# Moving weight preparation out of a state-space stage: where side work stands in the engines' queues

## The chip, the cores and the metric

The kernel runs on one core of a Trainium2 chip. The core has a matrix engine (PE, whose weight loads are listed apart as PEld), a vector engine (DVE), a scalar engine (ACT), a general engine (POOL) and an engine that here only issues transfers (SP). Each engine works through its own instructions in a fixed order and waits on semaphores for the others; transfers run on DMA engines and are issued from the queue of an engine, here SP or ACT. The metric is the device time of one execution in microseconds. A comparison of two kernels uses the median of several executions on the same chip.

## The reference: what is computed

One decoder block over 1024 positions of width 1024, in fp32. Two branches read one normalised input; they are merged by gates and projected. Then come a cross-attention into 256 memory tokens and a gated feed-forward.

```python
u = rms_norm(h, norm_mix[l])
proj = u @ w_in[l]                       # u_ssm, q, k, v, f_logit, gate_logits
y_ssm = gelu(s5_ssm(u_ssm, ...))         # state space
glu_a, glu_b = split(y_ssm @ w_glu[l], 2)
out_a = glu_a * sigmoid(glu_b)
out_b = forgetting_attention(q, k, v, f_logit + b_forget[l]) @ w_fox_o[l]
gate_a, gate_b = split(sigmoid(gate_logits), 2)
h = h + (gate_a * out_a + gate_b * out_b) @ w_mix_out[l]
h = h + memory_cross_attention(...)
f_a, f_b = split(rms_norm(h, norm_ffn[l]) @ w_ffn_in[l], 2)
h = h + (silu(f_a) * f_b) @ w_ffn_out[l]
return rms_norm(h, norm_final)
```

## The kernel before, in words

Each fp32 operand of a product is held as two parts: a high part (an ACT copy in a narrower type, L177) and a low part (the rest, a subtraction on DVE, L178); `split` makes both. Each product is three matmuls (`mm3`, L167 to L169) of 128 by 128 weights by 512 columns. Weights come through `wblock`: a load by SP into `raw`, then a split into `whi` and `wlo`.

The stages, by the time at which they stand in the profile: the normalised input and first products (0 to about 100 us); the state-space stage `stage_ssm` (about 100 to 357); the forgetting attention (to about 645); the head of `stage_tail`, in which eight blocks of the gated unit (GLU), of the attention's output product and of the merge are computed in one loop over j (about 645 to 800); the memory attention; and the feed-forward, which multiplies 2 by 2 blocks with seven products of sums of blocks instead of eight products. Those sums are taken of the weights too, so each block j of the feed-forward needs its weights in seven prepared pieces, each in a high and a low part.

**The state-space stage.** 32 gate products (16 blocks by two halves, 24 matmuls each) run one behind the other on PE. Their sigmoids run on ACT (L479) and are stored to `gate_d` by a DMA from ACT's queue (L480). Between them stands the state-space work of four groups q, set by the dictionary `todo`: before gate product 4+7q `turn_weights(q)` (transposes L1405, products L1411, and three dependent transfers `Ts<-Ts` on SP, L1418), before 5+7q `states` (the load `xg<-u_d` on SP, L1429, and its products L1436), before 8+7q the ACT copy `Tt<-Ts` (L1423), before 9+7q `out` (products `pv<-xg,Tt` L1479 and L1480, and the activation `m<-pv` L1483) and `store` (`y_d<-yh`, `y_d<-yl` on SP). A second dictionary, `jobs`, hangs side work on the gate products. One kind is for the mixer, four times over: fetch two rows of blocks of `w_mix_out` into `wk` (two buffers), add and subtract them on DVE (L507), store to `sums_d` (L511). The other is for the first two blocks of the feed-forward (`AHEAD_IN = 2`): fetch two pieces of `w_ffn_in` into the same `wk` buffers (L516), add on DVE (L525), split into `wh` (three buffers), and store to `w_d` (L533). The feed-forward reads `w_d` at about 947 to 999 us (L890).

**The tail's loop.** For each j: a load of the GLU's weights, the value products and their copies on DVE (`sg<-mm`, L1162), the gate products with a sigmoid on ACT (`sb`, L1167) and a multiply on DVE (L1168), the state-space gate on POOL (L1175), then `fox_part(j)`: the product of the attention's output (PSUM bank `pv`), a gate and an add on DVE (`gb`, L612, and `sg<-sg,gb`, L613), splits into `A11`, and for j below 4 a subtraction, a split into `S3` and a store `am_d<-sg`.

**What sets the order.** A scheduler puts each engine's instructions into a fixed order before the launch. `tc.issue_after(ins)` holds what is written inside it behind `ins`, but only those instructions that are on the same engine as `ins`: with a mark on ACT, the DVE and SP instructions inside it are not held. In `stage_ssm` the mark is the gate's sigmoid, an ACT instruction:

```python
            with B.tc.issue_after(mark[-1].ins):   # L560
                for g in jobs.pop(i):
                    g()
```

Of the kernel before, what the change touches and what calls it, by code (L numbers as in the profile page):

```python
# [19 lines left out]
P = 128  # L20
# [270 lines left out]
AHEAD_IN = 2  # L291


@with_exitstack
def hybrid_block_kernel(ctx: ExitStack, tc: tile.TileContext, x, mem, norm_mix, w_in, b_forget,
# [19 lines left out]
    w_d = B.dram.tile([AHEAD_IN, 7, P, D], F32, name="w_d")  # L315
# [3 lines left out]
    with tc.tile_pool(name="ssm", bufs=1) as sp:  # L319
        s5 = S5(B, sp, lam_re[0], lam_im[0], log_dt[0], b_re[0], b_im[0], c_re[0], c_im[0], d_skip[0])  # L320
        with tc.tile_pool(name="xin", bufs=1) as xp:
            stage_in(B, xp, s5, x, mem, norm_mix[0], norm_mem_kv[0], w_in, w_mem_kv, uT, u_d, kv_d)
        with tc.tile_pool(name="qp", bufs=1, reuse_waits="tile") as qp:
            stage_ssm(B, s5, qp, uT, w_in, gate_d, u_d, y_d, w_mix_out, sums_d, w_ffn_in, w_d)
# [8 lines left out]
    with tc.tile_pool(name="st2", bufs=1, reuse_waits="tile") as s2:  # L333
        stage_tail(B, big, s2, sh, x, glu, aT, gate_d, kv_d, sums_d, w_d, w_fox_o, w_mix_out, norm_mem_q[0], w_mem_q,
# [125 lines left out]
def stage_ssm(B, s5, qp, uT, w_in, gate_d, u_d, y_d, w_mix_out, sums_d, w_ffn_in, w_d):  # L460
# [29 lines left out]
    V, mw, kept = B.V, {}, {}  # L490

    def wide():
        return [qp.tile([P, D], F32, tag="wk", bufs=2, name="wk") for _ in range(2)]

    def mix_fetch(k):
        mw[k] = wide()
# [16 lines left out]
    def ffn_fetch(j):  # L513
        mw["f", j] = wide()
        for w_, c in zip(mw["f", j], (0, FH)):
            S.dma_start(w_.rearrange("p (k c) -> p k c", k=8),  # L516
                        w_ffn_in[:, c + j * P:c + (j + 1) * P].rearrange("(k p) c -> p k c", p=P))

    def ffn_part(j, n):

        (a1, a2), (b1, b2) = [(w_[:, :512], w_[:, 512:]) for w_ in mw["f", j]]
        src, adds = {1: (a1, ()), 2: (a2, ()), 5: (a1, ((a2, b2), (a1, b1), (b1, b2))), 6: (a1, ((a2, a1), (a1, b2))),
                     7: (b1, ()), 3: (b2, ()), 4: (a2, ())}[n]
        for o, i in adds:
            V.tensor_add(o, o, i)  # L525
        kept[j, n] = [qp.tile([P, 512], F32R, tag="wh", bufs=3, name="wh") for _ in range(2)]
        B.split(*kept[j, n], src)

    def ffn_keep(j, n):
        i, h = {1: (0, 0), 2: (0, 1), 5: (2, 0), 6: (2, 1), 7: (4, 0), 3: (5, 0), 4: (5, 1)}[n]  # L530
        for m, t_ in enumerate(kept.pop((j, n))):
            o = 512 * (m if n == 7 else h)
# [22 lines left out]
    for i, f in enumerate(gates):  # L555
# [3 lines left out]
        if i in jobs:  # L559
            with B.tc.issue_after(mark[-1].ins):  # L560
                for g in jobs.pop(i):
                    g()


def stage_tail(B, big, s2, sh, x, glu, aT, gate_d, kv_d, sums_d, w_d, w_fox_o, w_mix_out, g_mq, w_mem_q, w_mem_o, g_ffn,
# [94 lines left out]

    for j in range(8):
# [3 lines left out]
        glu.rest(j)  # L665
        if j == 6:
# [472 lines left out]
class Glu:  # L1139
# [24 lines left out]
    def sigmoid(self, j, h):  # L1164
# [3 lines left out]
        self.B.V.tensor_mul(dst, dst, sb)  # L1168
# [717 lines left out]
```

## Time and profile before

| | us |
|---|---|
| median of 3 runs | 1619.14 (1617.86 to 1624.33) |
| the profiled execution | 1617.85 |
| its span, from the first to the last instruction | 1616.1 |
| PE busy in it | 1538.5 |
| DVE busy | 1071.5 |
| ACT busy | 670.2 |
| mean clock granted to PE | 0.975 |

The profiled execution took 1.75 us beside its span. A row of a timeline reads: start, length, engine, line, operation and tiles (out<-in), shape, count, and in brackets how long the engine had been idle before it and what it waited for. A row with "w_d<-wh" as releaser means that the landing of that store set it free. A row of the windows reads: stretch, length, then for PE, PEld, DVE, ACT and POOL the busy time with the count of instructions, then the clock granted to PE, the busy share of the DMA engines and GB/s.

### The profile page before, as it was taken

To read this page: it belongs to the slowest core of one execution; us is meant where nothing else is said; L and a number is where in the kernel's file an instruction comes from. 1 tells how busy PE (TensorE), PEld (TensorE's weight loads), DVE (VectorE), ACT (ScalarE), POOL (GpSimd) and SP (SyncE) were. 2 spreads that over 40 slices of the span, in tenths; PEclk is the share of its full clock that TensorE was granted. 3 is DMA by queue.
4 is the path that set the end of the run, shared out by engine and by line. 5 is a ranking of instruction groups with operands and counts; after the bars stand their busy time and mean duration, and the time that the engine had idled before them with its cause. 6 is when DMAs were issued, how large, how long until landed. Compare 5 with 4: busy or idle time off the path is not lost.

```text
span 1616.1 us, 20580 instructions
## 1 busy us (share of the span) xinstructions
PE 1538.5 (95%) x7301; PEld 1267.2 (78%) x7301; DVE 1071.5 (66%) x1902; ACT 670.2 (41%) x1193; POOL 237.7 (15%) x323
## 2 busy tenths in 40 slices
PE   6899799889999999999999998999999999999997
PEld 5688688779877667888878887888888888788886
DVE  5757666254477777878685687776776676466555
ACT  5522333332366664323355565333333333244342
POOL 3024434020011111410011210100010000000001
PEclk8999999899999989999999999999999999999999
DMA  8747654964113364556532168444445444796642
GB/s 261 150 99 180 198 139 146 190 193 125 14 35 56 61 167 138 180 178 218 186 92 79 66 208 316 152 151 150 156 157 168 158 150 145 263 391 230 196 157 104
DMA packets 204886, 258.70 MB, mean 160 GB/s; under 512 B 36248, under 2 KB 127288, under 8 KB 204272
## 3 DMA queue, kind: packets, MB, share of 16 engines
q1 hardware_dynamic: 200176, 249.01, 51.2%
q10 hardware_dynamic: 4608, 8.39, 1.4%
q8 instruction: 57, 0.93, 0.2%
q14 instruction: 45, 0.37, 0.1%
HBM read 176.08 MB, written 83.20 MB: 160 GB/s over the span
## 4 chain that ended last, share of the span: by engine, by line
PE 73%; DVE 9%; DMA 8%; POOL 3%; ACT 3%; issue 3%; SPq 1%; DVEq 0%; POOLq 0%; ACTq 0%
PE mm L943 15%; PE pv L943 7%; PE mm L167 6%; PE mm L169 6%; PE mm L168 6%; PE mm L1080 4%; PE sc L943 4%; PE sc L1080 3%; PE pv L1080 3%; DMA w_d<-wh 2%; PE mm L652 2%; PE sc L167 2%; PE sc L169 2%; PE sc L168 2%; PE misc L1080 1%
## 5 line engine op out<-in xcount | busy, mean ns | idle before, releaser
L178 DVE TENSOR_TENSOR wlo<-raw,whi 128x1024 fp32r<-128x1024 f32 (+2 forms) x126 | 134.1, 1067 | 109.4 <-ACT whi L177 108.9
L177 ACT CAST whi<-raw 128x1024 fp32r<-128x1024 f32 (+2 forms) x127 | 115.6, 914 | 143.8 <-PE mm L168 42.2
L167 PE MATMUL mm<-uh,whi 128*128 128x512 f32 x344 | 138.5, 403 | 3.0 <-ACT whi L177 3.0
L169 PE MATMUL mm<-uh,wlo 128*128 128x512 f32 x344 | 136.0, 396 | 0.4 <-DVE wlo L178 0.4
L168 PE MATMUL mm<-ul,whi 128*128 128x512 f32 x344 | 136.2, 396 | 0.0
L178 DVE TENSOR_TENSOR ol<-or,oh 128x1024 fp32r<-128x1024 f32 x73 | 89.3, 1223 | 70.7 <-ACT oh L177 69.6
L177 ACT CAST oh<-or 128x1024 fp32r<-128x1024 f32 x73 | 76.8, 1052 | 103.7 <-PE mm L1080 35.2
L975 POOL TENSOR_TENSOR g<-a,c 128x512 f32<-128x512 f32 x22 | 35.6, 1619 | 393.6 <-ACT a L974 374.1
L167 PEld LDWEIGHTS mm<-uh,whi 128*128 128x128 f32 x344 | 65.7, 191 | 15.5 <-ACT whi L177 3.5
L169 PEld LDWEIGHTS mm<-uh,wlo 128*128 128x128 f32 x344 | 65.5, 190 | 14.9 <-DVE wlo L178 1.5
L168 PEld LDWEIGHTS mm<-ul,whi 128*128 128x128 f32 x344 | 65.8, 191 | 11.0
L196 POOL TENSOR_TENSOR r<-ms,mhalf 128x1 f32<-128x1 f32 (+1 forms) x30 | 18.8, 629 | 374.8 <-DVE ms L192 345.8
L1705 POOL TENSOR_TENSOR pl<-pf,ph 128x512 fp32r<-128x512 f32 (+1 forms) x32 | 36.8, 1151 | 249.8 <-DVE ph L1704 204.7
L1702 ACT ACTIVATE pf<-sc 128x512 f32<-128x512 f32 (+1 forms) x96 | 46.4, 490 | 53.1 <-DVE sc L1698 31.1
L943 PE MATMUL pv<-S3h,we 128*128 128x512 f32 x176 | 58.1, 389 | 0.0
L167 PE MATMUL sc<-uh,whi 128*128 128x512 f32 x104 | 41.5, 399 | 0.0
L1080 PE MATMUL mm<-oh 128*128 128x512 f32 x106 | 41.2, 389 | 0.0
L1080 PE MATMUL mm<-ol,oh 128*128 128x512 f32 x106 | 41.2, 389 | 0.0
L1080 PE MATMUL mm<-oh,ol 128*128 128x512 f32 x106 | 41.2, 389 | 0.0
L1708 DVE TENSOR_TENSOR pl<-pf,ph 128x512 fp32r<-128x512 f32 (+2 forms) x64 | 35.5, 557 | 8.6 <-ACT ph L1707 7.8
L169 PE MATMUL sc<-uh,wlo 128*128 128x512 f32 x104 | 41.0, 394 | 0.0
L168 PE MATMUL sc<-ul,whi 128*128 128x512 f32 x104 | 41.0, 394 | 0.0
(675 smaller groups left out, 4594.6 us busy)
## 6 DMA issues: line engine op xcount, KB each, us to landing
or<-c_d SPq DMA_DIRECT2D x77, 256.0 KB
wo<-in_w_ffn_out_dram SPq DMA_DIRECT2D x22, 512.0 KB
c_d<-g SPq DMA_DIRECT2D x44, 256.0 KB
t_d<-wo SPq DMA_DIRECT2D x44, 256.0 KB
or<-t_d SPq DMA_DIRECT2D x44, 256.0 KB
raw<-in_w_ffn_in_dram SPq DMA_DIRECT2D x20, 512.0 KB
rawb<-in_w_ffn_in_dram SPq DMA_DIRECT2D x20, 512.0 KB
raw<-in_w_in_dram SPq DMA_DIRECT2D x18, 512.0 KB
```

What stands on the lines that cost most here:

```text
L167: T.matmul(ps, lh, rh, start=first, stop=False)
L168: T.matmul(ps, lh, rl, start=False, stop=False)
L169: T.matmul(ps, ll, rh, start=False, stop=last)
L177: self.A.copy(hi, src)
L178: (self.G if pool_lo else self.V).tensor_sub(lo, src, f32(hi))
L652: T.matmul(ps, l_[:, k, :], r_[:, k, :], start=n in (1, 2, 7) and kk == k == m == 0, stop=kk == k == 1 and m == 2, skip_group_check=True)
L943: T.matmul(ps, l_[:, k, :], r_, start=first and k == 0 and i == 0, stop=k == 3 and i == 2, skip_group_check=True)
L975: G.tensor_mul(g[:, 512:], a1, c1)
L1080: T.matmul(ps, l_[:, gi], r_[:, 512:], start=n < 3 and p == 0 and k == 0 or n == 7 and p == 0 and k == 0, stop=p == NP - 1 and k == 2, ski ...
L1702: self.exp = A.activation(pf[:, off:], ps[:, off:], AF.Exp)
L1705: G.tensor_sub(pl[:, off:], pf[:, off:], f32(ph[:, off:]))
L1708: V.tensor_sub(pl[:, off:], pf[:, off:], f32(ph[:, off:]))
```

## The change: what it does

The feed-forward's preparation leaves `stage_ssm` and its two dictionaries: four fetches of 512 KB, 14 ACT casts, 14 DVE subtractions, 10 DVE additions and 28 stores of 256 KB are gone from there. The mixer's jobs are hung on gate products 7k+2, 7k+3 and 7k+4 instead of 3k+3, 3k+4 and 3k+5. In `stage_tail` a function `ahead(j)` does the same preparation in the loop over j, in buffers of the tail's own pool (`wpr` holds the fetched weights, `wph` and `wpl` high and low parts): fetches by SP, sums on DVE, splits on ACT and DVE, and 14 stores of 512 KB issued by ACT. It is hung on a mark that is now the GLU's multiply on DVE (`self.mark`, L1192 of the changed kernel), so its DVE instructions are held behind that multiply, and its ACT and SP instructions are not. What `w_d` holds, and who reads it, stays.

```diff
@@ stage_ssm
     def mix_fetch(k):
-        mw[k] = wide()
+        mw[k] = [qp.tile([P, D], F32, tag="wk", bufs=2, name="wk") for _ in range(2)]
...
-    def ffn_fetch(j):
-        mw["f", j] = wide()
-        for w_, c in zip(mw["f", j], (0, FH)):
-            S.dma_start(w_.rearrange("p (k c) -> p k c", k=8),
-                        w_ffn_in[:, c + j * P:c + (j + 1) * P].rearrange("(k p) c -> p k c", p=P))
-
-    def ffn_part(j, n):
...
-        for o, i in adds:
-            V.tensor_add(o, o, i)
-        kept[j, n] = [qp.tile([P, 512], F32R, tag="wh", bufs=3, name="wh") for _ in range(2)]
-        B.split(*kept[j, n], src)
-
-    def ffn_keep(j, n):
...
-            S.dma_start(w_d[j, i + (m if n != 7 else 0)][:, o:o + 512], f32(t_))
-
     jobs = {}
     for k in range(4):
-        for i, f in ((3 + 3 * k, mix_fetch), (4 + 3 * k, mix_sums), (5 + 3 * k, mix_store)):
-            jobs.setdefault(i, []).append(lambda f=f, k=k: f(k))
-    for j in range(AHEAD_IN):
-        jobs.setdefault(15 + 8 * j, []).append(lambda j=j: ffn_fetch(j))
-        for i, n in enumerate((1, 2, 5, 6, 7, 3, 4)):
-            jobs.setdefault(16 + 8 * j + i, []).append(lambda j=j, n=n: ffn_part(j, n))
-            jobs.setdefault(17 + 8 * j + i, []).insert(0, lambda j=j, n=n: ffn_keep(j, n))
+        for i, f in ((7 * k + 2, mix_fetch), (7 * k + 3, mix_sums), (7 * k + 4, mix_store)):
+            jobs[i] = lambda f=f, k=k: f(k)
@@ stage_tail
+    def ahead(j):
+        def keep(n, t_):
+            A.dma_start(w_d[j, n], f32(t_))
+        def pair(n):
+            hl = slot(F32R, "wph"), slot(F32R, "wpl")
+            return hl, [[t_[:, o:o + 512] for t_ in hl] for o in (0, 512)]
+        def fetch():
+            pre[j] = [slot(name="wpr") for _ in range(2)]
+            for r_, c in zip(pre[j], (0, FH)):
+                S.dma_start(r_.rearrange("p (k c) -> p k c", k=8),
+                            w_ffn_in[:, c + j * P:c + (j + 1) * P].rearrange("(k p) c -> p k c", p=P))
+        def plain():
+            hl, _ = pair(0)
+            B.split(*hl, pre[j][0])
+            for i, t_ in enumerate(hl):
+                keep(i, t_)
+        def sums():
...
+            V.tensor_add(ra[:, 512:], ra[:, 512:], b22)
+            V.tensor_add(ra[:, :512], ra[:, :512], rb[:, :512])
+            V.tensor_add(rb[:, :512], rb[:, :512], b22)
+            B.split(*w5, ra[:, :512])
+            V.tensor_add(ra[:, 512:], ra[:, 512:], ra[:, :512])
+            V.tensor_add(ra[:, :512], ra[:, :512], b22)
+            B.split(*w6, ra[:, :512])
...
+    ahead0, ahead1 = ahead(0), ahead(1)
     for j in range(8):
...
         glu.rest(j)
+        with B.tc.issue_after(glu.mark.ins):
+            for f in {0: ahead0[:1], 1: ahead0[1:2], 2: ahead0[2:3], 3: ahead0[3:] + ahead1[:1], 4: ahead1[1:2],
+                      5: ahead1[2:3], 6: ahead1[3:]}.get(j, []):
+                f()
@@ class Glu, sigmoid
-        self.B.V.tensor_mul(dst, dst, sb)
+        self.mark = self.B.V.tensor_mul(dst, dst, sb)
```

How the change moves instructions shows in the order of each engine. PE's own order is the same in both kernels. Three places follow; line numbers of the changed kernel differ, so the same instruction has another number there.

SP, from the third of the mixer's four stores to the end of group 1's transfers (`sums_d<-wk` is a store of the mixer's sums, `xg<-u_d` the state-space input of group 1). Before:

```order
L511 DMA sums_d<-wk 128x512 x4
L498 DMA wk<-in_w_mix_out_dram 128x1024 x2
L153 DMA raw<-in_w_in_dram 128x4x256 x2
L511 DMA sums_d<-wk 128x512 x4
L516 DMA wk<-in_w_ffn_in_dram 128x8x128
L1429 DMA xg<-u_d 128x1024
L516 DMA wk<-in_w_ffn_in_dram 128x8x128
L1488 DMA y_d<-yh 128x1024
```

Now:

```order
L504 DMA sums_d<-wk 128x512 x4
L491 DMA wk<-in_w_mix_out_dram 128x1024 x2
L153 DMA raw<-in_w_in_dram 128x4x256 x2
L504 DMA sums_d<-wk 128x512 x4
L1453 DMA xg<-u_d 128x1024
L1512 DMA y_d<-yh 128x1024
```

The fetch for the feed-forward no longer stands ahead of `xg<-u_d`. The mixer's fetches and stores stand where they stood, although their jobs have other numbers: they are SP instructions, and the mark is on ACT. The mixer's 16 sums on DVE stand at the same rows as before, too.

ACT, around the copy `Tt<-Ts` of group 2. Before:

```order
L177 CAST wh<-wk 128x512
L480 DMA gate_d<-gs 128x512
L479 ACTIVATE gs<-mm 128x512
L177 CAST wh<-wk 128x512
L480 DMA gate_d<-gs 128x512
L1423 COPY Tt<-Ts 128x8x8x16
L479 ACTIVATE gs<-sc 128x512
L177 CAST wh<-wk 128x512
L480 DMA gate_d<-gs 128x512
L1483 ACT_TABLE_LOAD
```

Now:

```order
L475 ACTIVATE gs<-mm 128x512
L1447 COPY Tt<-Ts 128x8x8x16
L476 DMA gate_d<-gs 128x512
L475 ACTIVATE gs<-sc 128x512
L476 DMA gate_d<-gs 128x512
L1507 ACT_TABLE_LOAD
```

The casts of the feed-forward's weights, each of which stood ahead of the copy, of a gate's store or of the activations behind `out`, are gone.

ACT in the tail, from the sigmoid of j = 2, second half, on (`sb` is a sigmoid, `A11h` and `S3h` are casts of `fox_part`). Before:

```order
L1167 ACTIVATE sb<-mm 128x512 x2
L177 CAST whi<-raw 128x1024
L1167 ACTIVATE sb<-sc 128x512
L177 CAST A11h<-sg 128x512
L177 CAST S3h<-sg 128x512
L1167 ACTIVATE sb<-mm 128x512
```

Now:

```order
L177 CAST wph<-wpr 128x1024
L1191 ACTIVATE sb<-mm 128x512
L633 DMA w_d<-wph 128x1024
L633 DMA w_d<-wpl 128x1024
L177 CAST wph<-wpr 128x512
L1191 ACTIVATE sb<-sc 128x512
L177 CAST wph<-wpr 128x512 x4
L633 DMA w_d<-wph 128x1024 x2
L633 DMA w_d<-wpl 128x1024
L633 DMA w_d<-wph 128x1024
L633 DMA w_d<-wpl 128x1024
L177 CAST A11h<-sg 128x512
```

Six casts and seven stores of the first feed-forward block now stand between ACT's sigmoids of j = 2 and 3 and the first cast of `fox_part(0)`; the second block's follow in the same way over the later steps.

More of the change, by code (lines that the diff above doesn't have):

```diff
@@ L323, in hybrid_block_kernel @@
         with tc.tile_pool(name="qp", bufs=1, reuse_waits="tile") as qp:
-            stage_ssm(B, s5, qp, uT, w_in, gate_d, u_d, y_d, w_mix_out, sums_d, w_ffn_in, w_d)
+            stage_ssm(B, s5, qp, uT, w_in, gate_d, u_d, y_d, w_mix_out, sums_d)
     yT = Act(big, "big", 16, 4, L, name="y")
@@ L457, in stage_in, with stage_ssm @@
         acts[step[0]](step[1:])
-def stage_ssm(B, s5, qp, uT, w_in, gate_d, u_d, y_d, w_mix_out, sums_d, w_ffn_in, w_d):
+def stage_ssm(B, s5, qp, uT, w_in, gate_d, u_d, y_d, w_mix_out, sums_d):
     A, S = B.A, B.S
@@ L488, in weights @@
             s5.weights(q)
[L490 to L493 removed]
+    V, mw = B.V, {}
     def mix_fetch(k):
[L496 removed]
+        mw[k] = [qp.tile([P, D], F32, tag="wk", bufs=2, name="wk") for _ in range(2)]
         for w_, r_ in zip(mw[k], (k, 4 + k)):
@@ L560, in stage_ssm, with stage_tail @@
             with B.tc.issue_after(mark[-1].ins):
-                for g in jobs.pop(i):
-                    g()
-def stage_tail(B, big, s2, sh, x, glu, aT, gate_d, kv_d, sums_d, w_d, w_fox_o, w_mix_out, g_mq, w_mem_q, w_mem_o, g_ffn,
+                jobs[i]()
+def stage_tail(B, big, s2, sh, x, glu, aT, gate_d, kv_d, sums_d, w_fox_o, w_mix_out, g_mq, w_mem_q, w_mem_o, g_ffn,
                w_ffn_in, w_ffn_out, g_fin, out):
```

30 lines of the change are left out of this document (21 added, 9 removed).

## The prediction

> **What bounds the kernel now.** I read the page first: the busy times, then the chain of waits by line.
>
> ```profile
> span 1616.1 us, 20580 instructions
> PE 1538.5 (95%) x7301; PEld 1267.2 (78%) x7301; DVE 1071.5 (66%) x1902; ACT 670.2 (41%) x1193; POOL 237.7 (15%) x323
> PE mm L943 15%; PE pv L943 7%; PE mm L167 6%; PE mm L169 6%; PE mm L168 6%; PE mm L1080 4%; PE sc L943 4%; PE sc L1080 3%; PE pv L1080 3%; DMA w_d<-wh 2%; PE mm L652 2%; PE sc L167 2%; PE sc L169 2%; PE sc L168 2%; PE misc L1080 1%
> ```
>
> PE is busy for 1538.5 of 1616.1 us. No matmul goes, so only its 78 idle us, and what it loses to a lower clock, can be won. In the chain one transfer stands among PE's products: `w_d<-wh`, the store of the prepared feed-forward weights, with 2% of the span (some 32 us). That is the work that is moved. The windows say whether PE is idle in the two places touched:
>
> ```profile
> core 0: us, PE busy (x) PEld busy (x) DVE busy (x) ACT busy (x) POOL busy (x), PEclk, DMA share, GB/s
> 120.00:160.00 40.00, 40.00 (x198) 33.79 (x197) 29.04 (x43) 9.50 (x18) 19.60 (x42) 1.00 0.72 173
> 160.00:200.00 40.00, 33.03 (x167) 27.93 (x165) 25.55 (x41) 13.51 (x19) 19.75 (x44) 0.94 0.66 194
> 280.00:320.00 40.00, 33.49 (x152) 28.45 (x151) 12.12 (x23) 12.20 (x20) 0.00 (x0) 0.87 0.94 192
> 670.00:740.00 70.00, 70.00 (x311) 57.95 (x310) 51.77 (x59) 17.32 (x25) 14.96 (x11) 1.00 0.54 177
> 740.00:750.00 10.00, 10.00 (x46) 8.29 (x45) 10.00 (x16) 5.04 (x8) 0.00 (x0) 1.00 0.89 280
> ```
>
> Until 160 us PE is full, with the mixer's sums already running; later in the state-space stage it stands still and its clock is below 1.00; in the tail's loop it is full. PE's timeline has five gaps between 160 and 345 us, 24.4 us in all:
>
> ```profile
> 171.82 0.80 PE L1479 MATMUL pv<-xg,Tt 128*128 128x128 f32 x2 [3.15 <-ACT Tt L1423]
> 202.73 3.39 PE L1436 MATMUL pv<-xg,F 128*128 128x128 f32 x16 [6.56 <-DMA xg<-u_d]
> 275.41 0.49 PE L1479 MATMUL pv<-xg,Tt 128*128 128x128 f32 x2 [1.32 <-ACT Tt L1423]
> 296.67 1.09 PE L1405 MATMUL pv<-ident,fre 128*128 128x128 f32 x4 [6.51 <-ACT m L1483]
> 339.18 0.79 PE L1479 MATMUL pv<-xg,Tt 128*128 128x128 f32 x2 [6.84 <-ACT Tt L1423]
> ```
>
> Which of them the preparation causes is read from the timelines of SP, ACT and DVE just before:
>
> ```profile
> 186.38 5.32 SPq L511 DMA_DIRECT2D sums_d<-wk  x4
> 196.02 0.38 SPq L516 DMA_DIRECT2D wk<-in_w_ffn_in_dram  x1
> 196.49 0.53 SPq L1429 DMA_DIRECT2D xg<-u_d  x1
> ...
> 273.80 0.62 ACT L177 CAST wh<-wk 128x512 fp32r<-128x512 f32 x1 [4.51 <-DMA w_d<-wh]
> 294.00 0.62 ACT L177 CAST wh<-wk 128x512 fp32r<-128x512 f32 x1 [18.14 <-DMA w_d<-wh]
> 336.26 0.62 ACT L177 CAST wh<-wk 128x512 fp32r<-128x512 f32 x1 [12.82 <-DVE wk L525]
> ...
> 320.50 0.69 DVE L178 TENSOR_TENSOR wh<-wk,wh 128x512 fp32r<-128x512 f32 x1 [14.86 <-DMA w_d<-wh]
> ```
>
> For the gap at 202.73: SP was done with the mixer's stores at 191.70, stood until 196.02 at a fetch of the feed-forward's weights, whose `wk` buffer was still being stored, and only behind it issued `xg<-u_d`, which landed at 202.7. For those at 275, 297 and 339: ACT stood at a cast `wh<-wk` for 4.51, 18.14 and 12.82 us, twice for a buffer whose store had not landed, the third time for a DVE addition, itself queued behind DVE's 14.86 us wait for such a store. Behind the cast in ACT's order stood `Tt<-Ts`, or the activations that empty the PSUM bank. The gap at 171.82 comes before the first of these fetches, so it isn't the preparation's.
>
> **The change part by part.** *The mixer's sums* have other gate numbers, but their mark is an ACT instruction and they run on DVE and SP; their rows stand where they stood. I cost this at nothing, and the gap at 171.82 stays.
>
> *The preparation leaves the state-space stage.* The gain is four gaps, 6.56 + 1.32 + 6.51 + 6.84 = 21.2 us, and the time for which PE runs slowly behind them:
>
> ```profile
> 205.88 0.48 PE L167 MATMUL sc<-uh,whi 128*128 128x512 f32 x1
> 242.24 0.60 PE L1405 MATMUL pv<-ident,fre 128*128 128x128 f32 x4
> 244.81 0.48 PE L167 MATMUL mm<-uh,whi 128*128 128x512 f32 x1
> 279.01 0.47 PE L167 MATMUL mm<-uh,whi 128*128 128x512 f32 x1
> 301.68 0.77 PE L167 MATMUL sc<-uh,whi 128*128 128x512 f32 x1
> 302.25 0.63 PE L168 MATMUL sc<-ul,whi 128*128 128x512 f32 x1
> 344.17 0.48 PE L167 MATMUL sc<-uh,whi 128*128 128x512 f32 x1
> ```
>
> Transposes and small products of one group take 244.81 - 242.24 = 2.57 us without a gap and 301.68 - 296.67 = 5.01 behind one: 2.4 more; the matmuls after them are slow too (0.77 and 0.63 long, where the first of such a run is 0.48), for which I add 1.3. The 32 products of `out` take 279.01 - 275.41 = 3.60 behind the short gap and 344.17 - 339.18 = 4.99 behind the long one: 1.4 more. Behind 202.73, 16 products take 205.88 - 202.73 = 3.15 where half of 3.60 is 1.80: 1.4 more. Together 6.5, and 27.7 with the gaps.
>
> What is late next? `xg<-u_d` can go at 191.7. It took 6.2 us from its issue; by that it lands at 197.9, and PE is ready at 202.73 - 6.56 = 196.2: a gap of 1.7 us. Without the fetch beside it it may land sooner: from 0 to 2.5 with some slow products, and I take 1.5. At the other three places nothing in the order stands where the casts stood. The transposes of the earlier group at 242.24 had no gap, so I take 0.
>
> *The preparation enters the tail's loop*, which costs only what makes PE wait there. Its instructions have rows in the old place, and the 128x1024 forms in the loop itself:
>
> ```profile
> L178 DVE TENSOR_TENSOR wh<-wk,wh x14: 681/693/718, 238.1 to 351.1; 128x512 fp32r<-128x512 f32 x14
> L525 DVE TENSOR_TENSOR wk<-wk x10: 680/692/1778, 238.9 to 335.5; 128x512 f32<-128x512 f32 x10
> L177 ACT CAST whi<-raw 128x1024 fp32r<-128x1024 f32 x11 | 11.5, 1049 | 22.0 <-PE pv L168 9.5 <-PE mm L168 9.3 <-PE sc L168 3.2
> L178 DVE TENSOR_TENSOR wlo<-raw,whi 128x1024 fp32r<-128x1024 f32 x11 | 14.3, 1304 | 8.8 <-ACT whi L177 8.7
> ```
>
> Per block DVE gets one subtraction of 1.30, five of 0.69 and five additions of 0.69: 8.2 us, 16.4 for both blocks. ACT gets 1.05 + 5 x 0.62 = 4.1 (the cast at 294.00), 8.2 for both, and 14 DMA issues. From 670 to 740 us DVE is idle for 70 - 51.8 = 18.2 us and ACT for 52.7. So ACT has room, and DVE just enough, in pieces. On the DMA engines 14 stores and 4 fetches of 512 KB are 9.4 MB; at 177 GB/s for a share of 0.54 that is 29 us of the 32 that are free there. Where it bites first is the first attention part:
>
> ```profile
> 673.04 0.69 DVE L612 TENSOR_TENSOR gb<-gb,pv 128x512 f32<-128x512 f32 x1 [0.68 <-DMA gb<-gate_d]
> 679.10 0.33 SPq L620 DMA_DIRECT2D am_d<-sg  x1
> 681.77 0.33 SPq L598 DMA_DIRECT2D xm<-am_d  x1
> 683.30 0.39 PE L167 MATMUL pv<-ath,whi 128*128 128x512 f32 x1
> ```
>
> DVE empties PE's `pv` bank until 673.73, and PE wants it again at 683.30: 9.6 us of slack. In the new order all of the first block's DVE work, 8.2 us, stands ahead of that instruction, and so do ACT's casts with the fetch that they wait for. If the fetch lands with the sigmoid of the same step, DVE comes 8 to 11 us later: a cost of 0 to 1.5, and I take 1. The second block's work is spread over four steps with idle time in each; but DVE has none left at 740 to 750, so that a backlog still there would be paid: 0 to 2, and I take 1. Together 2; bounds 0, and above, where DVE's idle pieces take up nothing but one such slack, 16.4 - 9.6 = 6.8. A store of the same size landed here within 681.77 - 679.10 = 2.7 us, not the 15 to 18 of the state-space stage, and the tail's pool has 16 buffers where `wh` had three; so I do not expect the old holds.
>
> ```profile
> 670.12 2.25 DVE L1168 TENSOR_TENSOR sg<-sg,sb 128x512 f32<-128x512 f32 x1
> 685.50 1.16 DVE L1168 TENSOR_TENSOR sg<-sg,sb 128x512 f32<-128x512 f32 x1
> ```
>
> In the loop the same DVE multiply takes 1.16 or 2.25 us, and POOL is busy for 15.0 of the 70 us (the window above). The Trainium skill, in "SBUF — State Buffer", section "SBUF: two separate sides", has a rule that speaks against this place: DVE and GpSimd (POOL here) take one shared port pair as an exclusive lock, so that a DVE operation with two SBUF inputs waits until a GpSimd operation that reads SBUF has ended. The two lengths agree with it. By that rule the additions and subtractions, all with two inputs, would be lengthened where they meet POOL: an estimate from the rows is 15.0 / 70 of 16.4 us, 3.5 more on DVE, and the sum below would be 2 to 3 us higher.
>
> *The sum*, on the profiled execution of 1617.85 us (its span and 1.75 around it): 1617.85 - 27.7 + 1.5 + 2 = 1593.6. The median of the runs lies 1.3 above that execution, so 1595.
>
> **The rivals.** *The loop takes part of it back.* The stores that ACT issues wait for DVE's subtractions; ACT stands there, with the next sigmoid behind it, and DVE's multiply waits for that sigmoid, so that the two engines wait for each other by turns. For it: ACT's casts and stores are not held by the mark, and their rows stand between the sigmoids. Against it: 52.7 us of idle ACT. If each of seven steps loses 1 to 2 us beyond its slack, the cost is 7 to 14 instead of 2: 1600 to 1607.
>
> *Slower than before.* The holds of the state-space stage come back in the loop: with the DMA engines near full (9.4 MB more), a cast `wph<-wpr` waits 18 us for a buffer or its fetch, as the one at 294.00 did, and the sigmoid behind it waits. It decides from the point at which a hold is longer than the slack of 9.6: each costs 18 - 9.6 = 8.4 and 1.4 of slow products. To be slower than before takes four of the seven steps: 39 us, so 1595 - 2 + 39 = 1632. Against it: the 2.7 us of the store above.
>
> *The stage keeps other stalls.* The transfers `Ts<-Ts`, the weights' loads and `xg` remain on SP, and a chain of DVE work hidden by the stalls so far may show when PE arrives 20 us earlier. If half of the 27.7 us comes back, 1609. For it: the gap at 171.82 arose with no feed-forward work. Against it: the three causes are read in the queues, each with its wait.
>
> *The mixer's sums do spread out after all*, by transfers that land at other times, and the gap at 171.82 goes with its slow products: 3.2 + 1.4 less, 1590. Against it: their rows are the same.
>
> **How the numbers follow.** Forecast 0.66 (1588 to 1600), loop takes part back 0.17, stage keeps other stalls 0.09, sums spread 0.04, slower 0.04. The range that leaves out no more than 2 in 10 reaches from the case of the spread sums with a tail cost of 0 (1595 - 5 - 2 - 2 = 1586) to 1609. A measurement here tells about 0.5% (8 us) from no change: faster is below 1611, slower above 1627. Forecast, spread sums, the loop's part and most of the kept stalls are faster: 0.90; some of the last and a milder form of the holds are the same: 0.06; slower 0.04.
>
> **What would show it.** Right: in the changed profile PE is full from 200 to 345 us save for a gap below 2.5 us ahead of L1436's counterpart, the gap of about 3 us near 172 is still there, and PE stays full at clock 1.00 from 650 to 760. The transfer `w_d` is out of the chain. The prediction is wrong if PE waits in the loop for DVE's `gb` or for a sigmoid by more than a few us, if the gaps at the copies `Tt<-Ts` stay, or if the 3 us near 172 are gone.

## The result, and the profile after

Measured beside each other, the kernel before ran at a median of 1618.58 us (6 runs, 1616.15 to 1624.33) and the changed one at 1601.72 us (6 runs, 1597.43 to 1604.70): a ratio of 0.9892, with a 95% interval of 0.9871 to 0.9913. It is faster by 17 us, clear of the 0.5% that a measurement can tell; the forecast was 24 us, at 1595 in a range of 1586 to 1609. The profiled execution took 1597.43 us, the fastest of the six. Its page begins:

```profile
span 1595.6 us, 20523 instructions
PE 1527.3 (96%) x7301; PEld 1257.5 (79%) x7301; DVE 1067.9 (67%) x1900; ACT 669.6 (42%) x1191; POOL 247.9 (16%) x323
PE mm L967 14%; PE pv L967 7%; PE mm L167 6%; PE mm L169 6%; PE mm L168 6%; PE mm L1104 4%; PE sc L967 4%; PE sc L1104 3%; PE pv L1104 3%; PE sc L167 2%; PE sc L169 2%; PE sc L168 2%; PE mm L617 2%; PE misc L1104 1%; DMA Ts<-Ts 1%
```

PE has the same 7301 matmuls and is busy 11 us less, as fewer of them run at a lowered clock (its mean is 0.984, 0.975 before); its idle time fell from 77.6 to 68.3 us. The store of the prepared weights is out of the chain. PE's windows of the changed kernel, in the two places touched:

```profile
160.00:200.00 40.00, 34.86 (x183) 29.83 (x182) 25.68 (x42) 14.10 (x19) 19.09 (x44) 0.96 0.72 233
200.00:240.00 40.00, 40.00 (x207) 34.14 (x206) 24.88 (x36) 16.32 (x27) 15.79 (x40) 1.00 0.50 124
280.00:320.00 40.00, 40.00 (x215) 34.40 (x214) 16.91 (x20) 16.81 (x28) 5.54 (x9) 1.00 0.59 122
650.00:660.00 10.00, 10.00 (x46) 8.28 (x45) 10.00 (x15) 5.07 (x8) 5.72 (x2) 1.00 1.01 371
660.00:670.00 10.00, 7.55 (x34) 5.96 (x33) 8.98 (x11) 1.02 (x2) 5.18 (x2) 1.00 0.99 324
670.00:680.00 10.00, 10.00 (x38) 8.04 (x39) 5.01 (x6) 3.93 (x6) 0.00 (x0) 0.83 0.80 270
710.00:720.00 10.00, 7.16 (x32) 5.62 (x31) 7.79 (x10) 1.61 (x3) 2.50 (x2) 1.00 0.86 278
```

From 200 us on PE is full in the state-space stage, at clock 1.00. The tail's loop, full before, has now two holes and a stretch at 0.83. PE's timeline names the four gaps of both places:

```profile
172.11 0.79 PE L1503 MATMUL pv<-xg,Tt 128*128 128x128 f32 x2 [3.57 <-ACT Tt L1447]
198.13 2.02 PE L1460 MATMUL pv<-xg,F 128*128 128x128 f32 x16 [1.56 <-DMA xg<-u_d]
669.84 0.50 PE L167 MATMUL mm<-yh,whi 128*128 128x512 f32 x1 [2.45 <-DVE sg L1186]
715.85 0.50 PE L167 MATMUL pv<-ath,whi 128*128 128x512 f32 x1 [2.84 <-DVE gb L577]
```

The loop's two holes make 5.3 us; in the window at 0.83, behind the first, PE starts 38 matmuls, where a full one has 46.

Where the time went can be measured by stage, from marks that every kernel has: the first transposes of the state space, the first transpose behind the stage, and the attention's output products, whose first and last starts bound the tail's loop. Rows by tile, first of before, then of the changed kernel (count, least, median and longest ns, first and last start):

```profile
L1405 PE MATMUL pv<-ident,fre x16: 270/272/447, 136.8 to 297.3; 128*128 128x128 f32 x16
L1573 PE MATMUL misc<-ident,logf x8: 272/273/273, 390.3 to 392.6; 128*8 128x128 f32 x8
L167 PE MATMUL pv<-ath,whi x64: 389/389/389, 667.0 to 761.5; 128*128 128x512 f32 x64
L169 PE MATMUL pv<-ath,wlo x64: 389/389/389, 667.4 to 762.0; 128*128 128x512 f32 x64
```

```profile
L1429 PE MATMUL pv<-ident,fre x16: 270/272/273, 136.7 to 282.7; 128*128 128x128 f32 x16
L1597 PE MATMUL misc<-ident,logf x8: 272/272/273, 363.8 to 366.1; 128*8 128x128 f32 x8
L167 PE MATMUL pv<-ath,whi x64: 389/389/501, 637.3 to 739.3; 128*128 128x512 f32 x64
L169 PE MATMUL pv<-ath,wlo x64: 389/389/397, 637.8 to 739.8; 128*128 128x512 f32 x64
```

So the state-space stage (first mark to second) takes 253.5 before and 227.1 now, 26.4 less; the attention (to the first `pv<-ath`) 276.7 and 273.5; the loop 95.0 and 102.5, 7.5 more. These stretches serve below to compare kernels, because the medians carry some 3 us of scatter. "Held" is the mixer's jobs held in their places, an experiment below. Of one profiled execution of each kernel, in us, with the ratio of all runs beside it:

| kernel | state space | attention | loop | ratio to before (95%) |
|---|---|---|---|---|
| before | 253.5 | 276.7 | 95.0 | 1 |
| changed | 227.1 | 273.5 | 102.5 | 0.9892 (0.9871 to 0.9913) |
| changed, again | 227.7 | 273.5 | 103.4 | 0.9883 (0.9863 to 0.9903) |
| no preparation at all | 229.6 | 274.2 | 95.0 | 0.9856 (0.9841 to 0.9871) |
| no stores | 228.4 | 273.1 | 105.6 | 0.9902 (0.9887 to 0.9917) |
| no DVE work | 229.9 | 275.1 | 102.0 | 0.9875 (0.9856 to 0.9894) |
| neither | 228.9 | 277.1 | 96.0 | 0.9861 (0.9845 to 0.9877) |
| behind the attention part | 226.8 | 274.3 | 102.4 | 0.9890 (0.9870 to 0.9909) |
| mixer held | 223.1 | 273.1 | 104.0 | 0.9850 (0.9832 to 0.9869) |
| in the attention | 229.3 | 281.4 | 95.0 | 0.9873 (0.9855 to 0.9891) |
| in the attention, mixer held | 223.3 | 282.6 | 95.0 | 0.9844 (0.9822 to 0.9867) |
| the same, subtractions on POOL | 223.3 | 285.1 | 95.0 | 0.9870 (0.9854 to 0.9886) |
| one block there, one in the loop, held | 222.7 | 278.9 | 101.0 | 0.9867 (0.9847 to 0.9888) |
| one block only, in the attention, held | 224.1 | 280.6 | 95.0 | 0.9865 (0.9842 to 0.9888) |

### The profile page after: what moved, and what is told of

It is laid out like the page before. It is cut to its first block, busy times and chain, and to the rows that moved or that the text cites. A ratio compares the mean times of both kernels' runs of the same rounds, so it can differ in the third digit from the quotient of the medians.

```text
span 1595.6 us, 20523 instructions
## 1 busy us (share of the span) xinstructions
PE 1527.3 (96%) x7301; PEld 1257.5 (79%) x7301; DVE 1067.9 (67%) x1900; ACT 669.6 (42%) x1191; POOL 247.9 (16%) x323
## 4 chain that ended last, share of the span: by engine, by line
PE 75%; DVE 8%; DMA 8%; issue 3%; ACT 3%; POOL 2%; SPq 1%; DVEq 0%; POOLq 0%; ACTq 0%
PE mm L967 14%; PE pv L967 7%; PE mm L167 6%; PE mm L169 6%; PE mm L168 6%; PE mm L1104 4%; PE sc L967 4%; PE sc L1104 3%; PE pv L1104 3%; PE sc L167 2%; PE sc L169 2%; PE sc L168 2%; PE mm L617 2%; PE misc L1104 1%; DMA Ts<-Ts 1%
## 5 line engine op out<-in xcount | busy, mean ns | idle before, releaser
L196 POOL TENSOR_TENSOR r<-ms,mhalf 128x1 f32<-128x1 f32 (+1 forms) x30 | 19.9, 666 | 372.9 <-DVE ms L192 345.3
L1199 POOL TENSOR_TENSOR sg<-sg,ga 128x512 f32<-128x512 f32 x16 | 36.8, 2318 | 72.6 <-DVE sg L1192 50.8
L167 PE MATMUL mm<-yh,whi 128*128 128x512 f32 x104 | 41.8, 402 | 2.4 <-DVE sg L1186 2.4
L169 PE MATMUL mm<-yh,wlo 128*128 128x512 f32 x104 | 41.6, 400 | 0.0
L168 PE MATMUL mm<-yl,whi 128*128 128x512 f32 x104 | 41.4, 398 | 0.0
```

Source lines behind the costliest of these rows:

```text
L167: T.matmul(ps, lh, rh, start=first, stop=False)
L168: T.matmul(ps, lh, rl, start=False, stop=False)
L169: T.matmul(ps, ll, rh, start=False, stop=last)
L1199: self.B.G.tensor_mul(self.out[j][:, cs], self.out[j][:, cs], ga)
```

## The experiments

Theories at the start: (A) leaving the state-space stage is worth the 26 us of the prediction's sum, and the loop takes some 9 back; (B) the loop takes little, and the stage kept part of the gain. For the loop's cost: (C) the stores and the DMA engines; (D) DVE's work in front of the instructions that empty PE's banks.

### No preparation at all

```diff
         with B.tc.issue_after(glu.mark.ins):
-            for f in {0: ahead0[:1], 1: ahead0[1:2], ...}.get(j, []):
-                f()
+            pass
...
-        S.dma_start(f32(t_), w_d[j, n])
+        S.dma_start(f32(t_), sums_d[4 + n % 4, j])
```

> The changed kernel without any preparation of the first two feed-forward blocks: the loop's calls of ahead(j) are left out (no fetch, sums, splits or stores), and the feed-forward reads the mixer's stored sums in place of the prepared weights, so the transfers that it reads with stay, while the products of the first two feed-forward blocks are computed from other numbers. It measures both terms of the sum at once. Theory (the prediction's): leaving the state-space stage is worth 27.7 - 1.5 us, so this runs at 1618 - 26 = 1592, and the 9 to 10 us from there to the changed kernel's 1601.7 are what the tail's loop costs, not the 2 of the prediction. Rival: the loop costs the predicted 2, and the state-space stage or the attention kept the rest; then this runs at 1599 to 1600.

Measured 0.9856 (0.9841 to 0.9871), 1598.3 us beside 1621.9 of before on this chip. As a time alone that is nearer to the rival's 1599 than to 1592; the stretches tell the two apart. With the changed kernel's ratio this chip would give 1604.4, so the loop's work costs some 6 us in the medians, with an interval of some 4 to each side, and the loop's stretch returned to exactly 95.0: 7.5 us in the profiles, not 2. Theory A holds: the gain of the stage is 23.6 us in the median and 253.5 - 229.6 = 23.9 in the profiles, the loop takes 6 to 8 back. The absolute 1592 was missed because the kernel before ran 3 us longer here (1621.9, 1618.6 in the first measurement) and because this run's stage kept another gap:

```profile
191.00 0.77 PE L1427 MATMUL pv<-ident,fre 128*128 128x128 f32 x4 [4.30 <-ACT m L1505]
```

It has no gap near 172, and one of 4.3 us at 191 instead, although the order of the stage's instructions is that of the changed kernel. In the eight profiles of this order the stage takes 226.8 to 229.9 us. Five have the gap at the copy `Tt`, 2.25 to 3.57 us long; the other three have one of 4.05 to 4.76 at the activations `m` instead, and they are the three whose first stage was longest (140.0 to 141.5 us up to the first mark, 135.5 to 138.5 in the five). The gap ahead of the `xg` products is anything from less than 0.7 to 3.40 us in them.

### No stores

```diff
         def keep(n, t_):
-            A.dma_start(w_d[j, n], f32(t_))
+            pass
```

> The changed kernel with the 14 stores to w_d left out; fetches, casts, sums and subtractions stay in the loop, and the feed-forward reads the mixer's stored sums instead, so the products of its first two blocks come from other numbers. If the loop's cost comes from the stores (ACT standing at their issue with sigmoids and casts behind it, and 7.3 MB more on DMA engines that the changed trace shows at a share of 0.99 to 1.01 from 650 to 670 us, so that the GLU's weights and gates land late), this takes 1592 to 1595, within 3 us of the kernel without any preparation. If the cost comes from DVE's 16 us and ACT's 8 us of sums and splits, this stays at 1600 to 1602.

Measured 0.9902 (0.9887 to 0.9917), the loop 105.6: no gain at all. Theory C as the only cause falls, and with it the prediction's rival of sigmoids that wait behind ACT's stores. The trace shows what limits instead, first a window, then rows of the timelines of DVE, SP and PE in order of time:

```profile
650.00:660.00 10.00, 9.51 (x42) 7.53 (x41) 10.00 (x12) 3.01 (x5) 4.07 (x3) 1.00 0.65 189
```

```profile
664.24 0.70 DVE L583 TENSOR_TENSOR sg<-sg 128x512 f32<-128x512 f32 x1
664.97 0.34 SPq L585 DMA_DIRECT2D am_d<-sg  x1
666.14 0.99 SPq L153 DMA_DIRECT2D raw<-wg_d  x2
669.02 0.90 SPq L545 DMA_DIRECT2D gb<-gate_d  x2
675.14 0.69 DVE L577 TENSOR_TENSOR gb<-gb,pv 128x512 f32<-128x512 f32 x1 [3.70 <-DMA gb<-gate_d]
679.68 0.80 PE L167 MATMUL mm<-yh,whi 128*128 128x512 f32 x1 [5.73 <-DVE sg L1186]
```

DVE is full from 650 to 660 and comes late to the subtraction `sg<-sg` of `fox_part(0)`. SP stands at the store `am_d<-sg` of its result, and behind it in SP's order stand the next weights and the gates `gb`. They are issued at 666 to 669, DVE waits for the gates until 675, and PE for the copy `sg` behind them, 5.7 us. Counted from the first product of the attention's output, this store is issued at 21.9 us, in the changed kernel at 21.5, and in the kernel before at 12.1.

### No DVE work

```diff
         def plain():
-            B.split(*hl, pre[j][0])
+            A.copy(hl[0], pre[j][0])
             for i in range(2):
+                keep(i, hl[0])
...
-            V.tensor_add(ra[:, 512:], ra[:, 512:], b22)
...
-            B.split(*w5, ra[:, :512])
+            A.copy(w5[0], ra[:, :512])
```

> The changed kernel with DVE's share of the preparation left out: no additions and no subtractions; the high part is stored in the place of both parts, the seventh piece is two ACT casts, so that fetches, ACT's casts and all 14 stores stay (the weights of the first two feed-forward blocks are other numbers then). Leaving out the stores had changed nothing. If it is DVE's 16 us, standing ahead of the instructions that empty PE's banks, that make the loop's cost, the cost goes: ratio to the kernel before 0.985 to 0.987, as without any preparation. If it is the fetches, ACT's casts between the sigmoids or the buffers, the ratio stays at 0.988 to 0.991.

Measured 0.9875 (0.9856 to 0.9894), beside 0.9883 for the unaltered kernel; the loop 102.0. Theory D as the only cause falls as well. Here PE waits once, 4.9 us for `gb`, with DVE at leisure. The same window, and the timelines of SP, DVE and PE:

```profile
650.00:660.00 10.00, 9.53 (x43) 7.55 (x41) 4.35 (x4) 3.30 (x6) 2.84 (x3) 1.00 1.05 377
```

```profile
648.65 4.39 SPq L642 DMA_DIRECT2D wpr<-in_w_ffn_in_dram  x2
653.14 5.41 SPq L545 DMA_DIRECT2D gb<-gate_d  x2
663.70 0.69 DVE L577 TENSOR_TENSOR gb<-gb,pv 128x512 f32<-128x512 f32 x1 [7.37 <-DMA gb<-gate_d]
664.44 0.79 PE L167 MATMUL pv<-ath,whi 128*128 128x512 f32 x1 [4.91 <-DVE gb L577]
```

The DMA engines' share is 1.05. The two issues for the gates take 5.4 us on SP, behind the two for a fetch of the second block, which take 4.4; the gates land at 663.7. In the kernel before, the rows of the first three such pairs are 2.13, 0.90 and 1.18 us long, with SP's waits between the two issues in them.

### Neither

```diff
         def keep(n, t_):
-            A.dma_start(w_d[j, n], f32(t_))
+            pass
...
-            B.split(*hl, pre[j][0])
+            A.copy(hl[0], pre[j][0])
```

> The changed kernel with both of its loads taken away at once: no stores to w_d and no DVE additions or subtractions of the preparation; the fetches and ACT's casts stay (the weights of the first two feed-forward blocks come from other numbers). Leaving out either alone left the loop's length, from the first to the last product of the attention's output, at 102 to 106 us, against 95.0 without the preparation. If either load alone is enough to make the loop's cost, because the one delays the gates' and weights' loads in the DMA engines and the other delays the store on SP that stands ahead of them, the loop falls to 95 to 97 here and the ratio to 0.985 to 0.987. If the fetches or ACT's casts are the cause, it stays at 102 and more, and the ratio at 0.988 to 0.990.

Measured 0.9861 (0.9845 to 0.9877), the loop 96.0. So fetches and casts cost about 1 us, and the loop's 7.5 us come from two loads of which either alone is enough: DVE's work, which makes the store on SP late and with it the loads behind it, and the stores' traffic, with which the same loads are issued and land late. They do not add up: in each kernel PE's wait is for `gb` or for the copy `sg`. One limit of this proof stands in SP's order. In the kernel without DVE's work, and in this one, the second block's fetch stands ahead of the first gates `gb`; in the changed kernel and in the one without stores it stands behind them. So that the stores alone are enough is shown beside a fetch that the gates wait behind. The fetch by itself is not harmless either: here the issues for these gates still take 3.25 us, at a DMA share of 0.96, and DVE waits for them for 3.34 us, but PE doesn't.

### The changed kernel again, and the preparation behind the attention part

```diff
-        with B.tc.issue_after(glu.mark.ins):
-            for f in {0: ahead0[:1], ...}.get(j, []):
-                f()
...
+        m_ = fox_part(j - 3) if j > 2 else glu.mark    # the last add of gb
+        with B.tc.issue_after(m_.ins):
+            for f in {1: ahead0[:1], 2: ahead0[1:2], 3: ahead0[2:3], 4: ahead0[3:] + ahead1[:1], 5: ahead1[1:2],
+                      6: ahead1[2:3], 7: ahead1[3:]}.get(j, []):
+                f()
```

> The changed kernel itself, unaltered, beside the next three on their chip, since chips differ by some us. Both theories expect the ratio of the first measurement again, 0.987 to 0.991, some 17 us below the kernel before.

> The changed kernel with the preparation one step later and behind fox_part: its mark is the last add of gb on DVE instead of the GLU's multiply, so that gb and its add, which free PE's pv bank, stand ahead of it. DVE's work is the same. If the place in DVE's queue decides, the cost of the loop falls by half or more: ratio 0.985 to 0.988. If DVE simply has too little idle time in that stretch, the wait moves to the copies sg of the value products or to the mixer's start, and the ratio stays at 0.988 to 0.992.

The unaltered kernel gave 0.9883 (0.9863 to 0.9903), as the first time. One step later and behind `gb` gave 0.9890 (0.9870 to 0.9909), the loop 102.4. The wait moved to the copy `sg`, 2.2 us at 671.92, and to `gb`, 1.6 us at 719.88; this other place in DVE's queue gains nothing.

### The mixer truly held

```diff
-            with B.tc.issue_after(mark[-1].ins):
+            with B.tc.issue_after((B.last_sub if i % 7 == 3 else B.last_load).ins):
                 jobs[i]()
```

> The changed kernel with the mixer's jobs truly held: the fetches and stores on SP behind the last load of weights on SP, the sums on DVE behind the last weight subtraction on DVE, so that they spread over the gate products 7k+2 to 7k+4 as their numbers say. Theory: the gap of 3.6 us near 172 us (for the copy Tt) comes from the mixer's transfers, which stand on SP between the three Ts transfers; it and the slow products behind it go, and the time is 1601.7 - 5 = 1596 to 1597. Rival: the three Ts transfers are late by themselves, or the mixer's stores delay those of another group; then 1600 to 1604.

Measured 0.9850 (0.9832 to 0.9869), the stage 223.1. In the five profiles with this edit the stage takes 222.7 to 224.1 us, in the eight without it 226.8 to 229.9: about 5 us. SP's queue shows the reason, first in the changed kernel, then with the mixer held:

```profile
148.17 1.07 SPq L1442 DMA_DIRECT2D Ts<-Ts  x1
151.10 3.95 SPq L504 DMA_DIRECT2D sums_d<-wk  x3
160.97 0.57 SPq L1442 DMA_DIRECT2D Ts<-Ts  x1
161.66 1.75 SPq L491 DMA_DIRECT2D wk<-in_w_mix_out_dram  x2
164.20 0.51 SPq L1442 DMA_DIRECT2D Ts<-Ts  x1
```

```profile
151.45 0.64 SPq L1442 DMA_DIRECT2D Ts<-Ts  x1
152.14 4.12 SPq L491 DMA_DIRECT2D wk<-in_w_mix_out_dram  x2
164.48 4.98 SPq L1442 DMA_DIRECT2D Ts<-Ts  x2
171.31 1.05 ACT L1447 COPY Tt<-Ts 128x1024 f32<-128x1024 f32 x1 [2.80 <-DMA Ts<-Ts]
172.44 0.47 PE L1503 MATMUL pv<-xg,Tt 128*128 128x128 f32 x2
```

The first `Ts<-Ts` is issued 3.3 us later here, as this run's first stage was 4.0 longer, but the copy `Tt` starts at the same time in both, 171.01 and 171.31: from the first transfer to the copy it takes 19.9 us instead of 22.8, with no store of the mixer's and one pair of its fetches between the three transfers, and PE takes `Tt` up without a wait. Since three profiles of the unheld order with as long a first stage have no gap near 172 either, this pair alone would not prove it. The four later kernels with the mixer held do: with first stages of 137.2 to 139.0 us their gap there is at most 0.84, where the unheld order has 2.25 to 3.57 at 135.5 to 138.5. The gap at `m` is gone in all five too; why, no run tells apart. What the five have instead is a gap of 1.4 to 2.6 us ahead of the next group's `xg` products, at 241 to 244.

### The preparation in the attention

```diff
+        def part(j, n):
+            ...
+            with B.tc.issue_after(self.mark.ins):      # a DVE copy of the scores
+                for o, i in adds:
+                    V.tensor_add(o, o, i)
+            hl = [fp.tile([P, 512], F32R, tag="wh", bufs=2, name="wh") for _ in range(2)]
+            with B.tc.issue_after(self.exp.ins):       # the exponential on ACT
+                B.split(*hl, src)
...
             for i, u in enumerate(units):
                 self.scores(h, *u)
+                if prep and i in (2, 6, 10):
+                    prep.pop(0)()
```

> The same preparation in a third place: in the forgetting attention, two to three pieces per head over the first heads, its ACT casts held behind the exponential on ACT and its DVE additions behind a copy on DVE, the stores on SP, with a pair of buffers for one piece of 128 by 512. The changed trace shows the DMA engines at shares of 0.00 to 0.40 there (400 to 520 us) and PE at 19.5 to 20 of 20. If what costs time in the other two places is landing times and queues, this runs within 4 us of the kernel without any preparation, at 1592 to 1596, and beats both kernels. If DVE, busy for 15 to 18 of 20 us in that stage, or ACT has no room, PE waits there and this takes 1600 to 1610.

> The preparation in the forgetting attention together with the mixer's jobs truly held, each of which alone ran at 0.987 and 0.985. If the two gains are of different stages, as their traces say (the gap near 172 us in the one, PE full in the tail's loop in the other), they add up but for what the attention pays: held is worth 6 to 7 us against the changed kernel, so 0.982 to 0.984, the fastest of all. If the mixer's spread transfers push the state-space stage's others, 0.985 to 0.988.

Alone 0.9873 (0.9855 to 0.9891), with the mixer held 0.9844 (0.9822 to 0.9867). Alone it ran within 1 us of the kernel without preparation on the same chip (1599.2 and 1598.3 us), but not at the 1592 to 1596 expected. The loop is back at 95.0, and the attention pays 281.4 and 282.6 instead of 273.1 to 277.1: as much as the loop did. PE's longest waits there, with the mixer held, are for DVE's reductions of the row maxima (`mc`) and for ACT's exponentials and their high parts (`pf`, `ph`), each short (us in total, times, longest):

```profile
PE mm L1638 <- DVE mc L1643: 4.3, 5, 1.2
PE sc L1665 <- ACT pf L1672: 3.0, 6, 0.7
PE pv L1690 <- ACT ph L1677: 3.0, 2, 2.5
```

From 400 to 520 us the DMA engines are at a share of 0.32 and DVE is busy for 99 of the 120 us, where without the preparation it is 90; a wait for `mc` comes once in the changed kernel, with 0.6 us. That points at DVE, but the second variant below does not bear it out. The last of these kernels has the lowest ratio of all, but its interval overlaps that of the mixer held alone (0.9832 to 0.9869): which of the two is faster can't be told. Against the unaltered kernel on the same chip (0.9883, 0.9863 to 0.9903) it is 6 us faster in the median, with intervals that overlap by a hair.

### Variants of it

One block there, one in the loop, the mixer held:

```diff
-        for j in range(AHEAD_IN):
+        for j in range(1):                     # in the attention: block 0
             todo.append(lambda j=j: fetch(j))
...
+            for f in {0: ahead1[:1], 2: ahead1[1:2], 4: ahead1[2:3], 6: ahead1[3:]}.get(j, []):   # in the loop: block 1
+                f()
```

> The first feed-forward block prepared in the attention, the second in the tail's loop (fetch at j = 0, pieces at j = 2, 4 and 6), with the mixer's jobs truly held. Each place pays some 7 us for both blocks. If that cost is a backlog beyond what a stage has free, half the work costs less than half, 1 to 2 us in each place: the attention's stretch 276 to 278 us, the loop's 95 to 98, ratio 0.981 to 0.983, faster than all others. If each piece costs the same wherever it stands, nothing is gained over both blocks in the attention: 0.984 to 0.985.

Both blocks in the attention, subtractions on POOL, the mixer held:

```diff
-                B.split(*hl, src)
+                B.split(*hl, src, pool_lo=True)
```

> Both blocks in the attention and the mixer's jobs held, as in the run at 0.9844, but the 14 subtractions on POOL instead of DVE. In that run PE's waits in the attention were for DVE's reductions of the row maxima and for the splits of the exponentials. If DVE's time is what the attention pays with, taking 9.7 of its 16.6 us off wins 3 to 4 us: the attention's stretch 278 instead of 282.6, ratio 0.982. If POOL's operations block DVE's, or delay POOL's own splits of the exponentials, the stretch stays at 282 or grows, ratio 0.984 to 0.987.

One block in the attention, the other not prepared ahead, the mixer held:

```diff
-AHEAD_IN = 2
+AHEAD_IN = 1
...
+    w_fetch(1)
     w_sums(0)
     start(0)
```

> Both blocks in the attention with the mixer's jobs held ran at 0.9844 and paid 8 us in the attention. Here only the first block is prepared ahead (in the attention); the second is fetched and split in the feed-forward itself, like the blocks after it, so no 14 stores and loads of its pieces. If half the work costs the attention about half (278.9 us in the run with one block there, against 282.6) and the feed-forward's start hides the second block's 8 us of DVE work behind its products, 0.981 to 0.983. If the feed-forward's start, where PE already stands for a few us, has no room for it, its stretch from the last attention product on grows by 4 to 8 us and the ratio is 0.984 to 0.988.

None gained: 0.9867, 0.9870 and 0.9865, with intervals of 0.002 to each side. One block in the loop still cost 101.0 - 95.0 = 6.0 there, where both cost 9.0 with the mixer held (104.0), and the other some 4 in the attention: half the work costs more than the 1 to 2 us expected. With the subtractions on POOL the attention took longer (285.1); 5.2 us of that are a wait for a projection's weights `whi`, which is 2.0 to 5.4 long in eleven other kernels and missing in the two just above, so no gain shows and no loss is settled. DVE was busy for only 93 of the 120 us from 400 to 520 there, so that DVE's time is what the attention pays with isn't shown. With one block only, the attention took 280.6, and from the last attention product to the end the time was 858.5 us (1595.4 less the 736.9 at which that product starts), where with both blocks ahead it was 858.1 (1597.3 - 739.2). As this last stretch lies anywhere from 854.1 to 858.6 in the thirteen other profiles, whose feed-forward runs the same instructions, these runs can't tell what preparing the second block ahead is worth to the feed-forward.

## Why the prediction was right or wrong

**The stage that is left: right, in each step and in size, with some luck.** The sum had 27.7 - 1.5 = 26.2 us; the profiles show 26.4. Against the other profiles of the same order it would have been 23.6 to 26.7, so the agreement to 0.2 is luck. The three gaps at 275, 297 and 339 are gone with their slow products. The gap ahead of the `xg` products was costed at 1.5 and is 1.56 in this profile, with no slow products behind it (16 in a row of 2.02 us, where the kernel before has 3.39). The gap near 172 stayed, 3.57 after 3.15, because the mixer's jobs did not move, as their rows said.

**The tail's loop: the mis-sized term.** I put it at 2 us with 6.8 as the upper bound; it is 7.5 and 8.4 in two profiles. The step that failed is the one that compared DVE's work with DVE's idle time (16.4 against 18.2 us) and the DMA engines' traffic with their free time (29 against 32 us) as if each were free to be used anywhere. Both were nearly used up in the mean, and locally nothing was left: DVE at 10.00 of 10 and the DMA engines at 1.01 from 650 to 660. The first attention part went as forecast: DVE comes to `gb` 14.8 us after the first output product instead of 6.1, some 9 later, within the slack of 9.6, and PE doesn't wait there. The cost comes behind it. PE's first hole is for the copy `sg` at 669.84: it stands in DVE's queue, and DVE is busy from 640.5 us on, but for 0.9 us at the next gates. The second goes through SP: a store of a late result, the gates issued behind it, DVE's wait for them.

```profile
707.15 0.32 SPq L585 DMA_DIRECT2D am_d<-sg  x1
709.74 6.94 SPq L545 DMA_DIRECT2D gb<-gate_d  x5
715.11 0.69 DVE L577 TENSOR_TENSOR gb<-gb,pv 128x512 f32<-128x512 f32 x1 [2.06 <-DMA gb<-gate_d]
```

I had not counted SP's queue in that step, though the change puts two fetches ahead of the gates there and the order showed it. Of the signs named in advance, PE full at clock 1.00 from 650 to 760 failed. The time lies just outside the forecast's own 1588 to 1600 and is that of the rival "the loop takes part of it back" (1600 to 1607, to which I gave 0.17); its mechanism, sigmoids behind ACT's stores, was not the cause, as the kernel without stores shows.

**The rule on the shared port.** The Trainium skill, in "SBUF — State Buffer", section "SBUF: two separate sides", let me estimate 3.5 us of lengthening on DVE. The trace agrees in part: three of the ten additions ran 1.72, 1.78 and 1.77 us instead of 0.68, each beside a POOL product, 3.2 us together. The subtractions were not lengthened: three from 650.27 on take 1.88 us together, within a POOL row that reaches from 649.24 to 655.72.

```profile
641.82 3.76 POOL L1199 TENSOR_TENSOR sg<-sg,ga 128x512 f32<-128x512 f32 x2 [4.49 <-DVE wpl L178]
...
642.72 1.72 DVE L655 TENSOR_TENSOR wpr<-wpr 128x512 f32<-128x512 f32 x1
644.35 1.78 DVE L656 TENSOR_TENSOR wpr<-wpr 128x512 f32<-128x512 f32 x1
646.16 0.69 DVE L657 TENSOR_TENSOR wpr<-wpr 128x512 f32<-128x512 f32 x1
```

That the lengthening set the loop's length isn't shown: without DVE's work the loop was as long.

**The median.** I added the 1.3 us by which the median of before lay above its profiled execution; for the changed kernel it is 4.3. The sum for the profiled execution was 1593.6, measured 1597.4: the loop's 5.5 too little, less 3.2 that the attention took less in this profile, and 1.5 in the rest. The 3.2 are scatter (without preparation there the attention takes 273.1 to 277.1) and hid part of the error by luck. The other 3 us between forecast and median are that scatter.

**Slower than before, and the kept stalls:** neither came in this profile; the gap at `m` in three others of the same order is a mild form of the second. The holds of 18 us did not return; that the tail's 16 buffers, which put room between a store and the next use, are the reason was not tested.

## What to carry to other kernels

Side work that stalls a stage is worth the stalls that stand in the queues behind it, and these can be read and added up; but the place it goes to must be costed where it lands, not by the mean idle time of its engines: look for the queue (here SP's) in which a load stands behind a store of a result that the moved work makes late. When two loads each suffice for a wait, taking away one shows nothing; take away both before calling either innocent. And a hold that names an instruction of one engine does not hold the others' instructions: each engine's order shows whether a move has happened at all.

## What was not expected of the hardware

The first stage, the same in all kernels, takes 135.5 to 141.5 us to the first state-space transposes. A wait of PE at the small operand `prow`, for nothing that the profile names ("issue"), goes along with it: 2.92, 3.53, 6.04, 6.98, 7.34 and 8.31 us in six profiles, the longest three in those whose first stage is 140.0 or more. PE's timeline of the kernel before, and of the one without stores:

```profile
72.21 0.23 PE L1228 MATMUL misc<-ident,prow 48*128 48x48 f32 x1 [3.53 <-issue]
```

```profile
76.36 0.31 PE L1252 MATMUL misc<-ident,prow 48*128 48x48 f32 x1 [8.31 <-issue]
```

A stretch that no change touches thus differs by 6 us between runs, as much as the effects in question, which is why stretches between marks were compared here. And DMA engines at a share near 1 went with long issues in SP's queue (5.4 us for two in the kernel without DVE's work, 3.25 in the one without stores too), and everything behind them in that queue came later.
